# A hybrid attention / mLSTM / HGRN2 backbone in two layers: a 32-byte tile at the right-hand end of SBUF

## The chip, the core and the metric

The kernel runs on one core of one Trainium2 chip. The metric is the device time of one execution in microseconds (us). Three runs of the kernel before took 3481.38, 3482.13 and 3482.68 us; their median, 3482.13 us, is the time before.

## The reference

Two layers over 1024 latent tokens and 256 context tokens of width 1024, in fp32. Cut to what matters here:

```python
def reference(x, c, ctx, c_ctx, ...):
    for l in range(DEPTH):                      # DEPTH = 2
        need_ctx = l < DEPTH - 1
        shift, scale, gate = _ada(c, w_ada[l], b_ada[l])
        h_lat = _rms(x, norm_w[l]) * (1.0 + scale) + shift
        h_ctx = _rms(ctx, norm_w[l]) * (1.0 + scale_c) + shift_c
        if l % 2 == 0:      # neighbourhood attention || bidirectional mLSTM
            y_lat, y_ctx = _ab_mixer(h_lat, h_ctx, w_in_ab[j], ...)   # h @ w_in, heads, ... @ w_out
        else:               # bidirectional HGRN2, 16 heads
            y_lat, y_ctx = _c_mixer(h_lat, h_ctx, w_in_c[j], ...)
        x = x + gate * y_lat
        if need_ctx:
            ctx = ctx + gate_c * y_ctx
    return x
```

Each mixer projects the normed and modulated stream `h` (1280 x 1024) onto 9,232 or 10,240 columns, works on the heads, and projects the result back with `w_out`.

## The kernel before

**Split matmuls.** Each large product is made of three: a matrix is split into a high part rounded to the fp32r type and a low part that holds the rest (`split`, L70 to L73: ScalarE writes the high part, VectorE the low one). `dense` (L125 to L131) issues per 128 rows of the contraction high x high (L128), high x low (L129) and low x high (L130), or the like, into one PSUM bank; `out_sum` (L829 to L837) does the same for the output projections (L835 to L837). Each of these matmuls has a stationary operand of 128 x 128 (loaded by an LDWEIGHTS of its own) and a moving operand of 128 x 256 or 128 x 512. In the profile's rows the moving operand stands first behind the arrow: `mm<-hh,wh` streams `hh` past a stationary `wh`.

**Two ends of SBUF.** Tiles come from pools. [...] Right-hand are:

- `hh` and `hl` (`open_h`, L251 to L254), the two parts of `h`, 40,960 bytes each, in both layers;
- pool `oy` (L1289 in layer 0, L1375 in layer 1) for the output projections: weight slabs `wol`, `woh`, the parts of the activations `yl`, `yh`, staging tiles `woraw` and `wraw`, sums `oacc`;
- pool `w1` (L1332), the ring of weight slabs `wl`, `wh` of layer 1.

Left-hand are the ring of layer 0 (`wl`, `wh` in pool `w0`), `wxl`, `wxh` of the wide projections, `wgl`, `wgh` of the gates, `wzl`, `wzh` of layer 1 (pool `hg`), the slabs of pool `wo1` (`wol`, `woh` of the last stages and of the second half of layer 0's output projection), and all tiles of the heads.

As the program is built, every right-hand tile begins 32 bytes behind a multiple of 64 (`hh` of layer 0 at byte 147,424, `hl` at 188,384). The left-hand weight slabs begin at multiples of 64, and so do the slices of them that matmuls read. (Some left-hand tiles of the attention begin 32 bytes behind one; the change leaves them there.) So a matmul that streams a left-hand slab past a stationary slice of `hh`, or the other way round, has one operand at a multiple of 64 and one 32 bytes behind; in this text such a matmul is called **mixed**. One with both operands on one side is called **same**.

**Stages**, in us from the start of the profiled execution:

- 0 to 265: modulation, `hh` and `hl`, first projections, gates;
- 265 to 1105: neighbourhood attention, with the projections of the next heads (`na_qk`, `na_z`, `proj_out`, `proj_out_tr`) between its small matmuls. `proj_nat` (L134) holds a slice of `hh` and streams the weights, 256 wide; `proj_tr` (L143) holds the weights and streams `hh`, 512 wide for the latents, 256 for the context. All of them are mixed;
- 1105 to 1590: mLSTM, with wide projections (`proj_wide`, L275: weights streamed 512 wide, mixed) laid between;
- 1590 to 1865: output projection of layer 0. In its first part six of eight slabs are left-hand and the activations right-hand (mixed), two slabs right-hand (same); later all is same;
- 1865 to 3277: HGRN2 over 16 heads. `hg_proj` (L882) streams `hh` past slabs of pool `w1`, both right-hand (same); `hg_vz` (L912) streams `wzl`, `wzh` past `hh`, 256 wide (mixed); the rest is left-hand;
- 3277 to 3481: output projection of layer 1, at first same, then with slabs of `wo1` (mixed, L1400 to L1406).

**Order.** The order of the instructions on each engine is laid down when the program is built. In `build` (L1154) the constants are loaded first; L1219 opens the right-hand stack with `hh` and `hl`.

Of the kernel before, what the change touches and what calls it, by code (L numbers as in the profile page):

```python
# [9 lines left out]
F32 = mybir.dt.float32  # L10
# [8 lines left out]
P = 128  # L19
# [25 lines left out]
class Prog:  # L45
# [1108 lines left out]
    def build(self):  # L1154
        tc, nc, a = self.tc, self.nc, self.a
        dma = nc.sync.dma_start
        with ExitStack() as es:
# [58 lines left out]
            )  # L1216


            right = ExitStack()  # L1219
            es.enter_context(right)  # L1220
            self.open_h(right)
# [76 lines left out]
            with tc.tile_pool(name="op0", bufs=2) as op, ExitStack() as wl:  # L1298
# [32 lines left out]
                right = es.enter_context(ExitStack())  # L1331
# [292 lines left out]
```

## Time and profile before

| | |
|---|---|
| median of three runs | 3482.13 us |
| span of the profiled execution, first to last instruction | 3480.9 us |
| TensorE (PE) busy | 3431.2 us, 99% |
| VectorE (DVE) busy | 2307.4 us, 66% |
| ScalarE (ACT) busy | 1488.6 us, 43% |
| GpSimd (POOL) busy | 725.6 us, 21% |

The span is that of one execution; what lies around it (launch and end) is 1.2 us if that execution was like the median one. A matmul's time in the profile is modelled from its start to the end of its pipeline, so matmuls that follow each other overlap: what one costs in a stream is the time from its start to the start of the next, which the timeline gives. Rows of "one line's instructions" give minimum/median/maximum time of one in ns, then the first and the last start; rows of groups give the busy time, the mean of one, and the idle time before them.

### The profile page before, as it was taken

To read this page: it belongs to the slowest core of one execution; us is meant where nothing else is said; L and a number is where in the kernel's file an instruction comes from. 1 tells how busy PE (TensorE), PEld (TensorE's weight loads), DVE (VectorE), ACT (ScalarE), POOL (GpSimd) and SP (SyncE) were. 2 spreads that over 40 slices of the span, in tenths; PEclk is the share of its full clock that TensorE was granted. 3 is DMA by queue.
4 is the path that set the end of the run, shared out by engine and by line. 5 is a ranking of instruction groups with operands and counts; after the bars stand their busy time and mean duration, and the time that the engine had idled before them with its cause. 6 is when DMAs were issued, how large, how long until landed. Compare 5 with 4: busy or idle time off the path is not lost.

```text
span 3480.9 us, 60852 instructions
## 1 busy us (share of the span) xinstructions
PE 3431.2 (99%) x22668; PEld 3042.3 (87%) x22668; DVE 2307.4 (66%) x5447; ACT 1488.6 (43%) x3577; POOL 725.6 (21%) x1076
## 2 busy tenths in 40 slices
PE   8999999999999999999999999999999999999997
PEld 5779998889989888898888999999999999999876
DVE  4546665666655566787666676667677677666767
ACT  5445554554544444455354333333333333333442
POOL 2222222222111112221110122122223222111125
PEclk9999999999999999999999999999999999999999
DMA  5542222322233434444752111111112211111274
GB/s 205 173 132 59 81 76 74 91 79 75 79 87 99 147 117 127 133 128 148 223 158 68 49 58 55 56 58 58 58 55 64 64 59 57 41 34 34 83 233 154
DMA packets 331527, 333.34 MB, mean 96 GB/s; under 512 B 30984, under 2 KB 277960, under 8 KB 331232
## 3 DMA queue, kind: packets, MB, share of 16 engines
q1 hardware_dynamic: 291008, 222.76, 21.7%
q0 software_dynamic: 40224, 106.69, 9.0%
q8 instruction: 179, 2.93, 0.4%
q14 instruction: 116, 0.95, 0.1%
HBM read 259.40 MB, written 69.79 MB: 95 GB/s over the span
## 4 chain that ended last, share of the span: by engine, by line
PE 89%; DVE 3%; issue 3%; DMA 2%; ACT 1%; POOL 1%; SPq 0%; POOLq 0%; ACTq 0%; DVEq 0%
PE mm L128 18%; PE mm L129 18%; PE mm L130 18%; PE s L1028 5%; PE mm L835 3%; PE mm L836 3%; PE mm L837 3%; PE acc L775 2%; PE tr L755 2%; PE acc L547 2%; PE s L556 2%; PE acc L537 1%; PE acc L1090 1%; PE acc L1088 1%; PE acc L1089 1%
## 5 line engine op out<-in xcount | busy, mean ns | idle before, releaser
L129 PE MATMUL mm<-hl,wh 128*128 128x512 f32 (+1 forms) x1600 | 587.1, 367 | 0.0
L128 PE MATMUL mm<-hh,wh 128*128 128x512 f32 (+1 forms) x1600 | 584.3, 365 | 0.0
L130 PE MATMUL mm<-hh,wl 128*128 128x512 f32 (+1 forms) x1600 | 583.7, 365 | 0.0
L128 PE MATMUL mm<-wh,hh 128*128 128x256 f32 (+1 forms) x1520 | 471.2, 310 | 1.2 <-ACT ev L317 0.6
L129 PE MATMUL mm<-wl,hh 128*128 128x256 f32 (+1 forms) x1520 | 469.9, 309 | 0.0
L130 PE MATMUL mm<-wh,hl 128*128 128x256 f32 (+1 forms) x1520 | 469.0, 309 | 0.3 <-DVE hl L262 0.3
L130 PEld LDWEIGHTS mm<-hh,wl 128*128 128x128 f32 x1600 | 301.6, 189 | 45.0 <-issue 0.5
L128 PEld LDWEIGHTS mm<-hh,wh 128*128 128x128 f32 x1600 | 301.4, 188 | 44.6 <-issue 0.3
L129 PEld LDWEIGHTS mm<-hl,wh 128*128 128x128 f32 x1600 | 301.6, 189 | 43.7 <-issue 0.2
L128 PE MATMUL mm<-wzh,hh 128*128 128x256 f32 x1024 | 299.7, 293 | 2.3 <-DVE gq L909 1.4
L128 PEld LDWEIGHTS mm<-wh,hh 128*128 128x128 f32 x1520 | 286.5, 189 | 16.0 <-issue 1.1
L129 PEld LDWEIGHTS mm<-wl,hh 128*128 128x128 f32 x1520 | 286.5, 188 | 14.7 <-issue 3.0
L130 PEld LDWEIGHTS mm<-wh,hl 128*128 128x128 f32 x1520 | 286.4, 188 | 13.8 <-issue 1.5
L130 PE MATMUL mm<-wzh,hl 128*128 128x256 f32 x1024 | 292.3, 285 | 0.0
L129 PE MATMUL mm<-wzl,hh 128*128 128x256 f32 x1024 | 292.0, 285 | 0.0
L72 ACT CAST wh<-wraw 128x512 fp32r<-128x512 f32 x240 | 147.3, 619 | 233.0 <-PE mm L129 175.8
L73 DVE TENSOR_TENSOR wl<-wraw,wh 128x512 fp32r<-128x512 f32 x240 | 164.8, 691 | 89.6 <-ACT wh L72 80.4
L1023 ACT COPY gksel<-gK 128x512 f32<-128x512 f32 x192 | 120.0, 633 | 218.2 <-PE s L1028 127.3
L1028 PE MATMUL s<-gQ,gksel 128*128 128x128 f32 x1536 | 203.9, 276 | 0.4 <-ACT gksel L1023 0.4
L128 PEld LDWEIGHTS mm<-wzh,hh 128*128 128x128 f32 x1024 | 193.4, 189 | 3.8 <-DVE gq L909 2.4
L129 PEld LDWEIGHTS mm<-wzl,hh 128*128 128x128 f32 x1024 | 193.6, 189 | 0.0
L130 PEld LDWEIGHTS mm<-wzh,hl 128*128 128x128 f32 x1024 | 192.7, 188 | 0.0
(400 smaller groups left out, 8017.5 us busy)
## 6 DMA issues: line engine op xcount, KB each, us to landing
wraw<-in_wab_dram SPq DMA_DIRECT2D x112, 256.0 KB
wraw<-in_wc_dram SPq DMA_DIRECT2D x96, 256.0 KB
wraw<-yd SPq DMA_DIRECT2D x94, 256.0 KB
adar<-in_wada_dram POOLq DMA_DIRECT2D x32, 512.0 KB, 4.4
wraw<-in_wc_dram SPq DMA_DIRECT2D x128, 128.0 KB
md<-ev POOLq DMA_DIRECT2D x60, 256.0 KB, 2.8
mloz<-md SPq DMA_DIRECT2D x40, 256.0 KB
adar<-in_wada_dram SPq DMA_DIRECT2D x16, 512.0 KB
```

The costliest lines, as they stand in the source:

```text
L72: nc.scalar.copy(hi, x)
L73: nc.vector.tensor_tensor(out=lo, in0=x, in1=hi.bitcast(F32), op=ALU.subtract)
L128: mm(ps, lhsT=lh(k), rhs=rh(k), start=(start and k == 0), stop=False)
L129: mm(ps, lhsT=lh(k), rhs=rl(k), start=False, stop=False)
L130: m = mm(ps, lhsT=ll(k), rhs=rh(k), start=False, stop=(stop and k == nk - 1))
L547: nc.tensor.matmul(num, lhsT=qc[:, j, :], rhs=C[d][:, j, :], start=False, stop=(j == 1))
L556: nc.tensor.matmul(u, lhsT=st["k"][c][:, j * P : (j + 1) * P], rhs=vw, start=True, stop=True)
L835: mm(ps, lhsT=yh[k], rhs=w.h(kk), start=(kk == 0), stop=False)
L836: mm(ps, lhsT=yh[k], rhs=w.l(kk), start=False, stop=False)
L837: mm(ps, lhsT=yl[k], rhs=w.h(kk), start=False, stop=(kk == 8 * len(qs) - 1))
L1023: nc.scalar.copy(ksel.rearrange("p (b s i) -> p b s i", s=2, i=h), pick(K))
L1028: nc.tensor.matmul(pa[:, c, :].rearrange("p (b s i) -> p b s i", s=2, i=h), lhsT=ksel[:, c * P : (c + 1) * P], rhs=qp[:, c * nbc : (c + 1) ...
```

## The change

Before `hh` and `hl` are opened, a pool `edge` on the right-hand side takes one tile of 8 fp32 (32 bytes) in each partition, for the whole program, and VectorE sets it to zero. Nothing reads it.

```diff
@@ -1216,6 +1216,8 @@
             )
 
 
+            edge = es.enter_context(tc.tile_pool(name="edge", bufs=1, side="right"))
+            nc.vector.memset(self.t(edge, [P, 8], F32, "edge"), 0.0)
             right = ExitStack()
             es.enter_context(right)
             self.open_h(right)
```

In the built program every other right-hand tile begins 32 bytes lower (`hh` of layer 0 at 147,392, `hl` at 188,352), at a multiple of 64; no left-hand tile moves. On each engine the same instructions stand in the same order, but for the one MEMSET more, the second instruction of work on VectorE. The waits are the same, with VectorE's count one higher.

## The prediction

> **What bounds the kernel now.** First the page: span, TensorE's busy time, and the chain of waits that ended last.
>
> ```profile
> span 3480.9 us, 60852 instructions
> PE 3431.2 (99%) x22668; PEld 3042.3 (87%) x22668; DVE 2307.4 (66%) x5447; ACT 1488.6 (43%) x3577; POOL 725.6 (21%) x1076
> PE 89%; DVE 3%; issue 3%; DMA 2%; ACT 1%; POOL 1%; SPq 0%; POOLq 0%; ACTq 0%; DVEq 0%
> PE mm L128 18%; PE mm L129 18%; PE mm L130 18%; PE s L1028 5%; PE mm L835 3%; PE mm L836 3%; PE mm L837 3%; PE acc L775 2%; PE tr L755 2%; PE acc L547 2%; PE s L556 2%; PE acc L537 1%; PE acc L1090 1%; PE acc L1088 1%; PE acc L1089 1%
> ```
>
> TensorE has 89% of the chain, 54% on the three lines of `dense` and 9% on those of `out_sum`. Next the busy times by stage (from:to, length, then PE, PEld, DVE, ACT, POOL busy, granted clock, DMA share, GB/s).
>
> ```profile
> 0.00:1590.00 1590.00, 1571.81 (x10814) 1368.47 (x10814) 979.47 (x2929) 769.31 (x1938) 346.79 (x586) 1.00 0.36 109
> 1590.00:1700.00 110.00, 107.51 (x482) 88.86 (x483) 79.74 (x200) 54.73 (x122) 14.98 (x26) 1.00 0.59 182
> 1700.00:1865.00 165.00, 164.01 (x783) 136.64 (x782) 100.93 (x229) 82.33 (x201) 16.85 (x36) 1.00 0.51 158
> 1865.00:3277.00 1412.00, 1409.31 (x9785) 1306.47 (x9784) 997.87 (x1877) 500.59 (x1162) 279.44 (x377) 1.00 0.17 52
> 3277.00:3481.00 204.00, 178.54 (x810) 141.82 (x807) 149.41 (x212) 81.63 (x156) 67.54 (x51) 0.96 0.63 197
> ```
>
> In every stage but the last TensorE is busy all but 1 to 2% of the time, at the full clock. So what matters of a change of addresses is whether matmuls that read right-hand tiles stream faster or slower.
>
> **The change part by part.** *The MEMSET* is the one new instruction. It comes between these two on VectorE:
>
> ```profile
> 0.80 0.07 DVE L1177 MEMSET mhalf<- 128x8 f32 x1 [0.80 <-PEq L1612]
> 2.75 0.18 DVE L1199 TENSOR_SCALAR sct<-sct 128x16 f32<-128x16 f32 x1 [1.88 <-ACT sct L1198]
> ```
>
> The same shape took 0.07 us, and VectorE then waits 1.88 us for ScalarE, which waits for a load. That hides it: 0. Without that cover, 0.07 us.
>
> *Who reads and writes right-hand tiles besides TensorE.* Splits into them are ScalarE casts; here one kind with all tiles left (`wzh`) and one with all right (`wh<-woraw`):
>
> ```profile
> L72 ACT CAST wzh<-wraw x64: 618/621/645, 1868.4 to 3200.1; 128x512 fp32r<-128x512 f32 x64
> L72 ACT CAST wh<-woraw x8: 616/622/627, 3283.1 to 3337.5; 128x512 fp32r<-128x512 f32 x8
> ```
>
> 621 and 622 ns: no difference of sides, so 0. DMAs into right-hand tiles (`woraw`, part of `wraw`) belong to the 2% that DMA has of the chain; no row tells their rate from that of others, and I take 0. PSUM isn't touched.
>
> *512-wide mixed matmuls.* Here the rows do differ. L836 by tile in three stretches (1590 to 1700, 1700 to 1865, 3360 to 3470), minimum/median/maximum in ns:
>
> ```profile
> L836 PE MATMUL mm<-wol,yh x57: 387/389/580, 1601.5 to 1700.0; 128*128 128x512 f32 x57
> L836 PE MATMUL mm<-wl,yh x54: 392/396/587, 1593.3 to 1672.1; 128*128 128x512 f32 x54
> ```
>
> ```profile
> L836 PE MATMUL mm<-wol,yh x182: 389/389/398, 1700.0 to 1844.5; 128*128 128x512 f32 x182
> L836 PE MATMUL mm<-wl,yh x20: 392/396/480, 1738.1 to 1846.8; 128*128 128x512 f32 x20
> ```
>
> ```profile
> L836 PE MATMUL mm<-wol,yh x129: 389/397/628, 3359.7 to 3469.5; 128*128 128x512 f32 x129
> L836 PE MATMUL mm<-wl,yh x4: 389/389/389, 3360.4 to 3362.4; 128*128 128x512 f32 x4
> ```
>
> Six groups of one line and one shape. In the first stretch `wl` is a left-hand slab under right-hand `yh` (mixed, 396) and `wol` right-hand (same, 389), and both take turns inside one accumulation. In the last the names change places: `wol` is left-hand (mixed, 397), `wl` right-hand (same, 389). So it is neither the tile nor the stage. Same on the left (most of the x182) and same on the right (x4) are both 389, so it isn't that a start 32 bytes off is slow in itself: the two operands' places within 64 bytes agree or they don't. After the change all of them agree.
>
> The price comes from the starts in unbroken streams; the first and last row of each: 40 matmuls with both sides left, then 32 mixed ones with `hh`:
>
> ```profile
> 1728.54 0.40 PE L836 MATMUL mm<-wol,yh 128*128 128x512 f32 x1
> ...
> 1737.42 0.39 PE L836 MATMUL mm<-wol,yh 128*128 128x512 f32 x1
> ```
>
> ```profile
> 258.68 0.39 PE L128 MATMUL mm<-hh,wh 128*128 128x512 f32 x1
> ...
> 265.90 0.39 PE L129 MATMUL mm<-hl,wh 128*128 128x512 f32 x1
> ```
>
> 8.88 us over 39 steps is 227.7 ns, 7.22 over 31 is 232.9: 5.2 ns less for each mixed one. How many there are (each row stands for three lines):
>
> ```profile
> L128 PE MATMUL mm<-wh,hh 128*128 128x256 f32 x1280 | 371.8, 291 | 1.2 <-ACT ev L317 0.6 <-ACT ev L634 0.3 <-ACT hh L261 0.2
> L128 PE MATMUL mm<-hh,wh 128*128 128x512 f32 x384 | 152.5, 397 | 0.0
> L128 PE MATMUL mm<-wh,hh 128*128 128x512 f32 x240 | 99.4, 415 | 0.0
> L128 PE MATMUL mm<-hh,wh 128*128 128x256 f32 x192 | 54.0, 281 | 0.0
> L128 PE MATMUL mm<-wxh,hh 128*128 128x512 f32 x80 | 32.5, 408 | 0.0
> ```
>
> ```profile
> L128 PE MATMUL mm<-wzh,hh 128*128 128x256 f32 x1024 | 299.7, 293 | 2.3 <-DVE gq L909 1.4 <-ACT gEc L921 0.5 <-ACT gz L934 0.4
> L128 PE MATMUL mm<-hh,wh 128*128 128x512 f32 x752 | 298.1, 396 | 0.0
> L128 PE MATMUL mm<-hh,wzh 128*128 128x256 f32 x128 | 35.9, 281 | 0.0
> ```
>
> The first fence is 0 to 1590 us, the second 1865 to 3277. Mixed and 512 wide: (384 + 240 + 80) x 3 = 2112 in layer 0, (54 + 20) x 3 = 222 in its output projection, 129 x 3 = 387 in the last stage: 2721, x 5.2 ns = **14.1 us less**. The ends: the x752 of HGRN2 are same already and yet have a mean of 396 like the mixed x384 (397), since other matmuls break their streams; if the attention's matmuls do that to layer 0 as well, nothing is gained. If each gains the whole 397 to 389, it is 21.8 us. I take 5.2: the unbroken stream of layer 0 is the row nearest to what changes.
>
> *256-wide mixed matmuls* are 7872: (1280 + 192 + 1024 + 128) x 3. Streams, first and last row: 75 rows of weights past `hh` (mixed), 23 of `hh` past weights (mixed), 19 in HGRN2 with both right (same), 63 of `wz` past `hh` (mixed):
>
> ```profile
> 276.98 0.28 PE L130 MATMUL mm<-wh,hl 128*128 128x256 f32 x1
> ...
> 285.74 0.28 PE L129 MATMUL mm<-wl,hh 128*128 128x256 f32 x1
> ...
> 270.43 0.28 PE L129 MATMUL mm<-hl,wh 128*128 128x256 f32 x1
> ...
> 272.99 0.28 PE L130 MATMUL mm<-hh,wl 128*128 128x256 f32 x1
> ...
> 2032.74 0.28 PE L129 MATMUL mm<-hl,wh 128*128 128x256 f32 x1
> ...
> 2034.89 0.28 PE L129 MATMUL mm<-hl,wh 128*128 128x256 f32 x1
> ...
> 1893.22 0.28 PE L130 MATMUL mm<-wzh,hl 128*128 128x256 f32 x1
> ...
> 1900.66 0.28 PE L129 MATMUL mm<-wzl,hh 128*128 128x256 f32 x1
> ```
>
> Per step: 8.76/74 = 118.4, 2.56/22 = 116.4, 2.15/18 = 119.4, 7.44/62 = 120.0 ns. Here agreement is no gain: if all come to 119.4, the 3840 of weights past `hh` lose 1.0 each (3.8 us), the 576 the other way round 3.0 (1.7 us), the 3072 with `wz` gain 0.6 (1.8 us), and the 384 `hh,wz`, for which I take 3.0 too, lose 1.2 us: **4.9 us more**. The ends: 0.6 gained by all (4.7 us less) and 3.0 lost by all (23.6 us more).
>
> *Sum.* 14.1 - 4.9 = 9.2 us less for TensorE. TensorE has 89% of the chain and what it saves elsewhere is met by other waits, so 8.2 us less of the span: 3480.9 to 3472.7. The median of the runs shown lies 1.2 us above this execution's span; with that, 3474 us. Between the ends of the two terms lie 26.5 us less and 23.6 us more.
>
> [...]
>
> **The rivals.**
>
> *Both at a multiple of 64 is better still than both behind it.* Then HGRN2's 752 x 3 matmuls, same before, would gain too: from a mean of 396 to the 389 of the x182, 7 ns, 15.8 us more. For it: the purest row is left-hand. Against: `wl,yh` x4, right-hand, has 389 as well, and broken streams explain the 396. With the sum: 0.89 x (9.2 + 15.8) = 22.3 us less, 3460 us; if half of it is so, 3467.
>
> *Nothing changes.* The 7 ns come from something that goes with the sides but isn't the place within 64 bytes, say the distance between the two operands; then the change doesn't do what it says: 3482 us. For it: no row has a right-hand tile at a multiple of 64. Against: the exchange of names above.
>
> *Slower: the 256-wide streams pay.* Operands that agree hold the 256-wide matmul at a longer period, and it is the more frequent form. If each of the 7872 loses the 3.0 ns that lie between 116.4 and 119.4, 23.6 us come in, mostly in the attention and in `hg_vz`, against 14.1 gained: 0.89 x 9.5 = 8.5 us more, 3491 us. It decides from 14.1 / 7872 = 1.8 ns each. For it: the 19 same ones have 119.4. Against: the `wz` streams (3072) are at 120.0 already.
>
> **How the numbers follow.** A difference under about 0.2% (7 us) is what a measurement of this kernel can't tell from no change. The forecast, 3474 us, has 0.62, with a range of its own of 3467 to 3480; its middle lies just beyond 7 us, but a share of the first rival's gain would add to it, so 0.45 of that is faster and 0.17 within. The first rival has 0.15 (faster), no change 0.09, slower 0.14. Faster 0.60, within 0.26, slower 0.14. The range of 3460 to 3486 takes in the first rival, no change and the near part of the third; it leaves out the third's own time and the outermost ends.
>
> **What would show it.** Right: L836's medians at 389 in all stretches, the stream near 258 us at about 228 ns a step, `mm<-hh,wh` x384 well under a mean of 397. The 256-wide streams near 277 us at 119 to 120 shows the toll; at 118.4 or less there is none. `wz` at 120.0 as before. Wrong: medians of 396 that stay; the x752 falling too (first rival); 256-wide steps over 120.2, 1.8 above 118.4 (third); or TensorE's busy time falling while the chain's share of DMA or VectorE grows by as much.

## The result, and the profile after

| | before | after |
|---|---|---|
| median of 19 runs each (us) | 3482.68 | 3476.21 |
| lowest to highest | 3479.62 to 3486.51 | 3471.94 to 3480.69 |
| span of the profiled execution | 3480.9 | 3472.7 |

The ratio of the times is 0.998, with a 95% interval of 0.9974 to 0.9986: 6.5 us less, a gain of 0.2% whose interval lies clear of no change. One execution among the experiments, the first profiled one of `minus64`, ran at a granted clock of 0.65 and took 4837 us; it is left out of the times below. From the page of the changed kernel, the span and the busy times:

```profile
span 3472.7 us, 60853 instructions
...
PE 3425.1 (99%) x22668; PEld 3046.3 (88%) x22668; DVE 2308.0 (66%) x5448; ACT 1486.9 (43%) x3577; POOL 727.0 (21%) x1076
```

TensorE is busy 6.1 us less than before and the span is 8.2 us shorter; VectorE, ScalarE and GpSimd each changed by less than 2 us. So the time went where it was looked for, in TensorE's matmuls. Next, where along the execution. The rows of two lines, first before, then after; "from to" are the first and the last start (L708: last small matmuls of the attention; L1028: HGRN2):

```profile
L708 PE MATMUL s<-akl,aqs x160: 278/282/386, 301.9 to 1141.2; 128*128 128x256 f32 x160
L1028 PE MATMUL s<-gQ,gksel x1536: 270/275/388, 1889.9 to 3279.6; 128*128 128x128 f32 x192
```

```profile
L708 PE MATMUL s<-akl,aqs x160: 274/283/385, 302.2 to 1140.7; 128*128 128x256 f32 x160
L1028 PE MATMUL s<-gQ,gksel x1536: 270/275/387, 1887.0 to 3272.1; 128*128 128x128 f32 x192
```

And L836 of the changed kernel in the first of the three stretches that the prediction shows (1590 to 1700 us), and in the last, here from 3340 to 3470 us, where the kernel before has a median of 397 as well:

```profile
L836 PE MATMUL mm<-wol,yh x60: 389/389/589, 1599.3 to 1699.5; 128*128 128x512 f32 x60
L836 PE MATMUL mm<-wl,yh x54: 389/394/587, 1591.2 to 1669.5; 128*128 128x512 f32 x54
```

```profile
L836 PE MATMUL mm<-wol,yh x136: 389/394/628, 3344.9 to 3461.2; 128*128 128x512 f32 x136
L836 PE MATMUL mm<-wl,yh x8: 389/389/389, 3347.6 to 3355.1; 128*128 128x512 f32 x8
```

The starts give the gain by stage, each beside the forecast for TensorE that the prediction's terms add up to:

| | how far earlier at its end | gained in it | forecast |
|---|---|---|---|
| to the end of the attention (last L708) | 0.5 us | 0.5 | |
| mLSTM, to the first L836 with `wl,yh` (1593.3, then 1591.2) | 2.1 | 1.6 | 5.5 for both |
| output projection of layer 0 (first L1028) | 2.9 | 0.8 | 1.2 |
| HGRN2 (last L1028) | 7.5 | 4.6 | 0.6 |
| last stage (last L836: 3469.5, then 3461.2) | 8.3 | 0.8 | 2.0 |

So the total was about right, but its place was not: more than half came in HGRN2, where almost nothing was forecast. L836 shows why the last stage gained less than forecast: the median of the slabs of `wo1` went from 397 to 394 ns, not to 389.

Groups of one shape of the changed kernel (busy us, mean ns), of 0 to 1590 us and of HGRN2:

```profile
L128 PE MATMUL mm<-wh,hh 128*128 128x256 f32 x1280 | 373.9, 292 | 1.0 <-ACT ev L317 0.6 <-ACT ev L634 0.3
L128 PE MATMUL mm<-hh,wh 128*128 128x512 f32 x384 | 151.0, 393 | 0.0
L128 PE MATMUL mm<-wh,hh 128*128 128x512 f32 x240 | 98.7, 413 | 0.2 <-ACT wh L72 0.2
```

```profile
L128 PE MATMUL mm<-wzh,hh 128*128 128x256 f32 x1024 | 299.5, 292 | 2.1 <-DVE gq L909 1.2 <-ACT gEc L921 0.5 <-ACT gz L934 0.4
L128 PE MATMUL mm<-hh,wh 128*128 128x512 f32 x748 | 296.1, 396 | 0.0
```

The mean of the x384 fell from 397 to 393 and that of the x240 only from 415 to 413. The 752 of HGRN2 (748 of them start in this window) stay at 396: the first rival did not happen. The streams of the prediction, again by the first and the last start (`hh` past `w`, `w` past `hh`, `wz` past `hh`):

```profile
258.80 0.40 PE L128 MATMUL mm<-hh,wh 128*128 128x512 f32 x1
...
265.85 0.39 PE L129 MATMUL mm<-hl,wh 128*128 128x512 f32 x1
...
276.87 0.28 PE L129 MATMUL mm<-wl,hh 128*128 128x256 f32 x1
...
285.98 0.28 PE L130 MATMUL mm<-wh,hl 128*128 128x256 f32 x1
...
1890.28 0.28 PE L130 MATMUL mm<-wzh,hl 128*128 128x256 f32 x1
...
1897.76 0.28 PE L130 MATMUL mm<-wzh,hl 128*128 128x256 f32 x1
```

7.05 us over 31 steps is 227.4 ns (232.9 before), 9.11 over 76 is 119.9 (118.4 before), 7.48 over 63 is 118.7 (120.0 before). These are single clean streams. For whole stages the following table has the mean time from a matmul's start to the next start, over all of that form that are followed within 260 ns (512 wide) or 150 ns (256 wide), worked out from the starts in both traces; below it is called the step.

| form, stage | steps | before | after |
|---|---|---|---|
| 512 wide, `h` past `w`, attention | 975 | 233.3 | 228.9 |
| 512 wide, `w` past `h`, mLSTM | 450 | 232.9 | 229.9 |
| 512 wide, `wo1` past `y`, last stage | 349 and 341 | 234.2 | 233.4 |
| 512 wide, `h` past `w`, HGRN2 | 2112 and 2099 | 229.5 | 228.9 |
| 256 wide, `w` past `h`, attention | 2143 and 2146 | 118.4 | 119.7 |
| 256 wide, `h` past `w`, attention | 504 | 117.3 | 119.5 |
| 256 wide, `wz` past `h`, HGRN2 | 2854 | 119.8 | 118.7 |

### The profile page after: what moved, and what is told of

Same layout as the page of the kernel before. It is cut to its first block, busy times and chain, and to the rows that moved or that the text cites. A ratio compares the mean times of both kernels' runs of the same rounds, so it can differ in the third digit from the quotient of the medians.

```text
span 3472.7 us, 60853 instructions
## 1 busy us (share of the span) xinstructions
PE 3425.1 (99%) x22668; PEld 3046.3 (88%) x22668; DVE 2308.0 (66%) x5448; ACT 1486.9 (43%) x3577; POOL 727.0 (21%) x1076
## 4 chain that ended last, share of the span: by engine, by line
PE 88%; issue 3%; DVE 3%; DMA 2%; ACT 1%; POOL 1%; SPq 0%; POOLq 0%; ACTq 0%; DVEq 0%
PE mm L128 18%; PE mm L129 18%; PE mm L130 18%; PE s L1028 5%; PE mm L835 3%; PE mm L836 3%; PE mm L837 3%; PE acc L775 2%; PE tr L755 2%; PE acc L547 2%; PE s L556 2%; PE acc L537 1%; PE acc L1089 1%; PE acc L1088 1%; PE acc L1090 1%
## 5 line engine op out<-in xcount | busy, mean ns | idle before, releaser
L129 PE MATMUL mm<-hl,wh 128*128 128x512 f32 (+1 forms) x1600 | 586.2, 366 | 0.0
L128 PE MATMUL mm<-hh,wh 128*128 128x512 f32 (+1 forms) x1600 | 582.8, 364 | 0.0
L130 PE MATMUL mm<-hh,wl 128*128 128x512 f32 (+1 forms) x1600 | 582.0, 364 | 0.0
L128 PE MATMUL mm<-wh,hh 128*128 128x256 f32 (+1 forms) x1520 | 472.6, 311 | 1.2 <-ACT ev L317 0.6
L129 PE MATMUL mm<-wl,hh 128*128 128x256 f32 (+1 forms) x1520 | 471.6, 310 | 0.0
L130 PE MATMUL mm<-wh,hl 128*128 128x256 f32 (+1 forms) x1520 | 471.0, 310 | 0.0
L130 PEld LDWEIGHTS mm<-hh,wl 128*128 128x128 f32 x1600 | 301.9, 189 | 43.3 <-issue 0.2
L128 PEld LDWEIGHTS mm<-hh,wh 128*128 128x128 f32 x1600 | 301.9, 189 | 43.1 <-issue 0.5
L129 PEld LDWEIGHTS mm<-hl,wh 128*128 128x128 f32 x1600 | 302.0, 189 | 41.6 <-issue 0.2
L128 PEld LDWEIGHTS mm<-wh,hh 128*128 128x128 f32 x1520 | 290.0, 191 | 15.3 <-issue 1.1
L129 PEld LDWEIGHTS mm<-wl,hh 128*128 128x128 f32 x1520 | 289.9, 191 | 14.3 <-issue 2.6
L128 PE MATMUL mm<-wzh,hh 128*128 128x256 f32 x1024 | 299.5, 292 | 2.1 <-DVE gq L909 1.2
L130 PEld LDWEIGHTS mm<-wh,hl 128*128 128x128 f32 x1520 | 290.0, 191 | 12.9 <-issue 1.5
L130 PE MATMUL mm<-wzh,hl 128*128 128x256 f32 x1024 | 292.2, 285 | 0.0
L129 PE MATMUL mm<-wzl,hh 128*128 128x256 f32 x1024 | 291.8, 285 | 0.0
L1023 ACT COPY gksel<-gK 128x512 f32<-128x512 f32 x192 | 119.9, 633 | 215.4 <-PE s L1028 118.8
L1028 PE MATMUL s<-gQ,gksel 128*128 128x128 f32 x1536 | 204.1, 276 | 0.2 <-ACT gksel L1023 0.2
L128 PEld LDWEIGHTS mm<-wzh,hh 128*128 128x128 f32 x1024 | 193.5, 189 | 3.5 <-DVE gq L909 2.2
L129 PEld LDWEIGHTS mm<-wzl,hh 128*128 128x128 f32 x1024 | 193.5, 189 | 0.0
L130 PEld LDWEIGHTS mm<-wzh,hl 128*128 128x128 f32 x1024 | 193.1, 189 | 0.0
```

Source lines behind the costliest of these rows:

```text
L128: mm(ps, lhsT=lh(k), rhs=rh(k), start=(start and k == 0), stop=False)
L129: mm(ps, lhsT=lh(k), rhs=rl(k), start=False, stop=False)
L130: m = mm(ps, lhsT=ll(k), rhs=rh(k), start=False, stop=(stop and k == nk - 1))
L1023: nc.scalar.copy(ksel.rearrange("p (b s i) -> p b s i", s=2, i=h), pick(K))
L1028: nc.tensor.matmul(pa[:, c, :].rearrange("p (b s i) -> p b s i", s=2, i=h), lhsT=ksel[:, c * P : (c + 1) * P], rhs=qp[:, c * nbc : (c + 1) ...
```

## The experiments

The starts within 128 bytes may explain what the table leaves odd, the `wo1` slabs' small gain (234.2 to 233.4 ns): after the change the layer-0 slabs and `hh` both begin 64 bytes behind a multiple of 128, but the slabs of `wo1` begin at a multiple of 128 and the activations 64 behind one. The start addresses here and below are those in the built programs. In all of them the uppermost right-hand tile ends at byte 229,344 (`hl` of the kernel before: 188,384 + 40,960), and each pool with `side="right"` lies below those that are open when it is opened, so a tile opened first moves all that come after it. There were four theories to begin with. A: the operands' places within 64 bytes must agree (the prediction's). B: within 128 bytes. C: right-hand tiles must begin at multiples of 64. D: any shift, or the MEMSET, does it. Each ratio below is against runs of the kernel before on the same chip.

**64 bytes in place of 32 (edge64).**

```diff
-            nc.vector.memset(self.t(edge, [P, 8], F32, "edge"), 0.0)
+            nc.vector.memset(self.t(edge, [P, 16], F32, "edge"), 0.0)
```

> The tile at the right-hand end has 64 bytes in place of 32: right-hand tiles begin 32 bytes behind a multiple of 64 as before, only 64 bytes lower than before; left-hand slabs are unmoved, so the mixed matmuls are mixed again. Theory A (the two operands' places within 64 bytes must agree) and theory B (their places within 128 bytes must agree): the 512-wide streams of layer 0 are back at 233 ns a step, L128 mm<-hh,wh of 265 to 1590 us back from a median of 389 to 393 or more, L836 mm<-wol,yh of the last stage at 396 or 397, and the time within 2 us of before, 3482.7. Theory C (what counts is that each right-hand tile begins at a multiple of 64): the same. Theory D (any shift, or the MEMSET itself, brings the gain): 3476 as in the changed kernel, medians of 389. One thing is open in A and B: the weights that stream past hh 256 wide now stand 32 bytes ahead of hh within 128, where before they stood 32 bytes short of it (before: 118.4 ns a step); the few that already had the operand that streams 32 ahead (hh past weights) took 116.4 to 117.4. If the sign matters to the 6912 matmuls of that form, 1 ns each is 7 us less, and the streams show it.

Measured: 3469.89 us, ratio 0.9963 (0.9951 to 0.9976). The 512-wide streams went back to 233 as A, B and C have it (`h` past `w` in the attention 232.9), so D falls. But the time is lower than that of the changed kernel, by the 256-wide streams. That of `w` past `hh`:

```profile
275.00 0.28 PE L129 MATMUL mm<-wl,hh 128*128 128x256 f32 x1
...
283.87 0.28 PE L130 MATMUL mm<-wh,hl 128*128 128x256 f32 x1
```

8.87 us over 76 steps is 116.7 ns, against 118.4 before and 119.9 after. The mean steps are 117.1 for `w` past `h` and 117.6 for `wz` past `h` (119.8 before): 3840 x 1.3 and 3072 x 2.2 ns are 11.8 us. The open point in the expectation was the larger effect: it matters whether the streamed operand lies 32 bytes ahead of the other or 32 short of it (the sign, below; for `w` past `h` 117.1 against 118.4 ns), which neither A nor B has.

**96 bytes (edge96).** The same line with [P, 24].

> The tile at the right-hand end has 96 bytes: right-hand tiles begin at multiples of 128, so at multiples of 64 as in the changed kernel, but the slabs of layer 0 and wz begin 64 bytes behind a multiple of 128, and the slabs of the last stage at a multiple of 128. Theory A (agreement within 64) and theory C (right-hand tiles at multiples of 64): as the changed kernel everywhere, 3476 us, L128 mm<-hh,wh of 265 to 1590 us at a median of 389, L836 mm<-wol,yh of the last stage at 394. Theory B (agreement within 128): the two trade places. Layer 0 is back at about 233 ns a step and a median of 393 or more, and the last stage falls from 394 to 389; 2100 matmuls lose what the change gave them and 400 gain, so the time lies at 3480 to 3484, unless the 256-wide streams take a step of their own at this distance. Theory D (any shift): 3476.

Measured: 3460.53 us, ratio 0.9934 (0.9920 to 0.9947), 22 us less than before. Streams, and L836 in the last stage:

```profile
257.38 0.39 PE L128 MATMUL mm<-hh,wh 128*128 128x512 f32 x1
...
264.61 0.39 PE L129 MATMUL mm<-hl,wh 128*128 128x512 f32 x1
...
275.37 0.28 PE L129 MATMUL mm<-wl,hh 128*128 128x256 f32 x1
...
283.98 0.28 PE L130 MATMUL mm<-wh,hl 128*128 128x256 f32 x1
```

```profile
L836 PE MATMUL mm<-wol,yh x136: 389/389/632, 3331.4 to 3445.4; 128*128 128x512 f32 x136
```

7.23 us over 31 steps is 233.2 ns: layer 0 lost its gain although every right-hand tile begins at a multiple of 64, and the last stage has 389 at last. For these two B is right and A and C are wrong. The time that B gave is wrong, by the reservation that stood with it: 8.61 over 76 is 113.3 ns for the 256-wide stream. Over whole stages `wz` past `h` fell to 115.3 and `w` past `h` to 117.2: 3072 x 4.5 and 3840 x 1.2 ns are 18.4 of the 22 us. For `w` past `h` a distance of 64 bytes is better than 0 (117.2 against 119.6 ns over all stages of the changed kernel).

**32 bytes on the left instead (left32).**

```diff
+            nc.vector.memset(self.t(cp, [P, 8], F32, "edge"), 0.0)
             right = ExitStack()
```

> No tile at the right-hand end; instead a 32-byte tile among the constants, so that every left-hand tile behind it moves up by 32 bytes and the right-hand ones stay where they were before. All operands of the mixed matmuls now begin 32 bytes behind a multiple of 64. Theories A and B (only agreement counts): as the changed kernel, 3476 us, L128 mm<-hh,wh of 265 to 1590 us at 389, and the last stage still at 394 since its slabs stand 64 bytes apart from the activations within 128. Theory C (a multiple of 64 is needed): no gain, 3482.7 or slower, medians of 393 or more. Theory D: 3476, with no pattern by stage.

Measured: 3476.27 us, ratio 0.9983 (0.9974 to 0.9991), as the changed kernel. The group of `h` past `w`, 512 wide, of 0 to 1590 us:

```profile
L128 PE MATMUL mm<-hh,wh 128*128 128x512 f32 x384 | 151.0, 393 | 0.0
```

The same 393 as after, with both operands 32 bytes behind a multiple of 64, and the last stage at 394 too. C falls: the gain came with the difference of the two places, not with either place.

**All dense matmuls at distance 0 within 128 bytes (all0).**

```diff
+                nc.vector.memset(self.t(pool, [P, 16], F32, "pad", 1), 0.0)
                 self.na_values(1, pool)
...
             with tc.tile_pool(name="op0", bufs=2) as op, ExitStack() as wl:
+                nc.vector.memset(self.t(op, [P, 16], F32, "pad", 1), 0.0)
...
                 wl1 = wl.enter_context(tc.tile_pool(name="wo1", bufs=1))
+                nc.vector.memset(self.t(wl1, [P, 16], F32, "pad", 1), 0.0)
```

> The changed kernel with three more tiles of 64 bytes in the left-hand pools (before the wide projection of the gates stage, in front of the second output projection of layer 0, in front of the slabs of the last stage), so that all dense matmuls have both operands at the same place within 128 bytes. Theory A (64 is enough): as the changed kernel, 3476 us, L836 mm<-wol,yh of the last stage stays at a median of 394. Theory B (128): this median falls to 389, the 504 matmuls concerned (384 of them in the last stage) lose about 5 ns each, 2 to 3 us in all: 3473 to 3475. A tile that moves by 64 bytes has no other price that the trace shows.

Measured: 3475.20 us, ratio 0.9976 (0.9967 to 0.9985). L836 in the last stage:

```profile
L836 PE MATMUL mm<-wol,yh x144: 387/389/632, 3328.7 to 3465.3; 128*128 128x512 f32 x144
```

394 became 389, as B has it. In the time, 1 us less than after is inside the intervals; the row shows the effect, the time doesn't settle it.

**wz alone (wz64).** The question was now whether 64 bytes between the operands make the 256-wide form fast (E), or the place of the right-hand tiles (F).

```diff
-            whole = [self.t(pool, [P, ns, 512], F32R, tag + c, 1) for c in "lh"]
+            x = 128 if tag == "wz" else 0
+            whole = [
+                self.t(pool, [P, ns * 512 + x], F32R, tag + c, 1)[:, x // 8 : x // 8 + ns * 512].rearrange(
+                    "p (s f) -> p s f", f=512
+                )
+                for c in "lh"
+            ]
```

> The changed kernel in which only wzl and wzh are moved, by 64 bytes (a view that begins 64 bytes into a slab that is 512 bytes longer); hh and hl stay. Theory E (256-wide matmuls run fastest when the streamed operand and the weights lie 64 bytes apart, slowest when they agree): HGRN2's streams of wz past hh fall from 118.8 ns a step to the 115.3 of the kernel with 96 bytes, all else stays; 3072 x 3.5 ns x 0.89 is 9.6 us, so 3467 us. Theory F (the gain of the 96 bytes came from right-hand tiles at multiples of 128, not from a distance): wz stays at 118.8 and the time at 3476.

Measured: 3465.46 us, ratio 0.995 (0.9938 to 0.9963), 11 us less than the changed kernel's median. The stream (six lines lower in the file, so L136 is L130):

```profile
1891.26 0.28 PE L136 MATMUL mm<-wzh,hl 128*128 128x256 f32 x1
...
1898.41 0.28 PE L136 MATMUL mm<-wzh,hl 128*128 128x256 f32 x1
```

7.15 us over 63 steps is 113.5 ns (118.7 after); the mean step is 115.1, and the forms without `wz` are as after. F falls, and E's forecast holds: 115.3 was expected.

**128 bytes (edge128).** The line of the first two experiments with [P, 32].

> The tile at the right-hand end has 128 bytes: every right-hand tile 128 bytes lower than before. Theory B (places within 128 bytes decide): no difference from before, 3482.7 us, 512-wide streams of layer 0 at 233 ns a step, w past hh at 118.4, wz past hh at 120.0. If the pattern is longer than 128 bytes, the 256-wide streams show other values (w stands 96 bytes ahead of hh now, before it stood 32 behind it).

Measured: 3482.34 us, ratio 0.9996 (0.9987 to 1.0005): the time of before, as B says. The streams say otherwise:

```profile
279.02 0.28 PE L129 MATMUL mm<-wl,hh 128*128 128x256 f32 x1
...
288.12 0.28 PE L130 MATMUL mm<-wh,hl 128*128 128x256 f32 x1
...
1901.63 0.28 PE L130 MATMUL mm<-wzh,hl 128*128 128x256 f32 x1
...
1909.08 0.28 PE L130 MATMUL mm<-wzh,hl 128*128 128x256 f32 x1
```

9.10 over 76 is 119.7 ns for `w` (118.4 before), 7.45 over 63 is 118.3 for `wz` (120.0 before). The two forms have exchanged their values, and 3840 x 1.2 ns more (4.7 us) hides 3072 x 1.6 ns less (4.9 us). In layer 0 the distance of `w` from `hh` went from 224 to 96 bytes within 256, and that of `wz` from 96 to 224. So the pattern is longer than 128 bytes, and B falls for this form; the exchange fits a length of 256, as do distances that differ by 256: `w` here, 96 bytes ahead of `hh`, has 119.6 over all stages, and `wz` before, 352 ahead within 512, had 119.8. The 512-wide streams, at 233 to 234, can't tell. An unchanged total was two changes that cancel.

**hh and hl 64 bytes apart (hsplit).** Does a step go with the matmul's own weights or with those that are loaded meanwhile? The next weights are loaded while a stream runs: in the kernel before, the LDWEIGHTS of L129 begins at 258.68 us as L128's matmul does, and that of L130 at 258.91 us as L129's does.

```diff
+        self.nc.vector.memset(self.t(self.hpool, [P, 16], F32, "pad", 1), 0.0)
         self.hl = self.t(self.hpool, [P, KD, T], F32R, "hl", 1)
```

> The changed kernel with a 64-byte tile between hh and hl, so that hh begins 64 bytes lower than in the changed kernel and hl stays. In the streams of wz (and of w, 256 wide) past h, three lines take turns: L128 streams past hh while hh is loaded for L129, L129 streams past hh while hl is loaded for L130, L130 streams past hl while the next hh is loaded. Theory G (the stream collides with the weights that are being loaded meanwhile): steps begun by L129 are slow (118.8 for wz, 119.6 for w), those begun by L128 and L130 fast (115.3 and 117). Theory H (a matmul's own two operands matter): those begun by L130 are slow, those of L128 and L129 fast. By both the 512-wide matmuls that stream hh past slabs at the old place go to 233 ns and those that stream hl stay at 227 to 229. Time by the sum of these, 9.9 us more for the 512-wide and 17 less for the 256-wide: about 3470; it doesn't tell G from H.

Measured: 3481.74 us, ratio 0.9996 (0.9987 to 1.0005), not 3470. Mean steps in ns by the line that begins them:

| form, stage | L128 | L129 | L130 |
|---|---|---|---|
| 256 wide, `w` past `h`, attention | 116.5 | 117.4 | 119.8 |
| 256 wide, `wz` past `h`, HGRN2 | 118.9 | 119.5 | 116.5 |
| 512 wide, `h` past `w`, attention | 234.4 | 234.9 | 229.9 |

H fits the first row, and neither fits the other two. In the second, the steps of L128 and L129, at distance 192, are slow, and that of L130, at 128, is not. In the third, streams of `hl` (L129), at distance 0, are slow and those of `hh` in L130, at 192, are not; the sum of the three is as if all stood at 192, so HGRN2's 2304 `h` past `w` gave back 4.4 ns each (10 us), where 7 us had been counted. The larger part of the miss is `wz`: the mean of its three steps is 118.3, 0.4 ns under the changed kernel, 1.3 us over 3072, where two thirds of them at 115.3 would have been 7 us. Two operand places in one accumulation are not the sum of the two cases. What collides, and whether anything does, stays open.

**The other sign, everywhere (minus64).** `lbm` goes, and `wz` moves by 128 bytes in its slabs (x // 4 in place of x // 8 in the edit of wz).

```diff
-            mx = self.t(cp, [P, 16], F32, "lbm")
+            mx = self.lb[:, 0, :]
```

> The changed kernel, in which the 64-byte tile lbm among the constants is gone (its place is taken by a half of lb that isn't in use yet) and wzl, wzh lie 128 bytes further into their slabs: the layer-0 slabs and wz begin 64 bytes below hh within 512, where in the kernel with 96 bytes the layer-0 slabs began 64 above it. Theory I (the sign counts: below is better for 256-wide weights that stream past h, above better for 512-wide): w past hh falls from 117 to about 115.3 (3840 matmuls), h past w 512 wide from 233 to 230 (1152), against 3 ns more for the 720 of w past hh 512 wide and 2 for the 576 of h past w 256 wide; 7 us less than with 96 bytes, x 0.89: 3454. Rival: the 115.3 belongs to wz and its stage, not to the sign; then w stays at 117 and the time at 3460 or a few us above.

Measured: ratio 0.9933 (0.9919 to 0.9946), 3458.5 to 3461.8 us in four executions. The steps come from a second profile of the same kernel.

> The same kernel as minus64, whose profile fell into an execution at a granted clock of 0.65 and tells nothing of the streams. Theory I: w past hh 256 wide at 115.3 ns a step (117 with 96 bytes), h past w 512 wide at 230 (233 with 96 bytes). Since the time, 3461 us, is that of the kernel with 96 bytes and not the 3454 forecast, at least one of the two must fail, or a stage lose by as much: the rival has w at 117 and h past w at 233.

Measured: 3460.02 us, ratio 0.9932 (0.9914 to 0.9950). Both halves of I hold: `w` past `h` in the attention has 115.7 and `h` past `w` 230.1. The loss is elsewhere: `wz` past `h` at 116.5, where wz64 had 115.1 with `wz` and `h` at the very same addresses. Here are two streams of one place in HGRN2, first of this kernel and then of the last experiment below:

```profile
1890.65 0.28 PE L135 MATMUL mm<-wzl,hh 128*128 128x256 f32 x1
...
1893.24 0.28 PE L136 MATMUL mm<-wzh,hl 128*128 128x256 f32 x1
```

```profile
1893.70 0.28 PE L135 MATMUL mm<-wzl,hh 128*128 128x256 f32 x1
...
1896.20 0.28 PE L136 MATMUL mm<-wzh,hl 128*128 128x256 f32 x1
```

Each has 22 steps: 117.7 and 113.6 ns. At this distance a stream takes one of two values, and the mean of a stage says how many took which. Counted over the 63 accumulations of `wz` past `h` of 24 matmuls each that run nearly unbroken, 38 have 113.3 to 114.2 and 25 have 117.6 to 117.9 in wz64, against 21 and 42 in minus64_again; none lies between. Is that chance? Two kernels were profiled once more for it.

> The kernel of wz64 once more. wz and hh stood at the same addresses there and in minus64_again, yet wz past hh took 115.1 ns a step in the one and 116.4 in the other. If the step varies from execution to execution, it may be anything between these here; if what else moved by 64 bytes in the left-hand pools makes the difference, it is 115.1 again (within 0.2).

> The changed kernel once more, for the same question: its streams repeat within 0.2 ns (w past hh 256 wide in the attention 119.7, wz past hh 118.7, hh past w 512 wide in the attention 228.9), or they vary by a nanosecond between executions and single steps can't be read so finely.

Measured: 3466.11 and 3474.59 us. Every mean step named repeats within 0.1 ns (`wz` 115.1 and 118.7, `w` 119.7, `h` past `w` 228.9). So it is not chance from execution to execution; the program decides.

**Layer 1 as in wz64 (minus64_l1).** What had moved with `minus64` besides was every other left-hand tile of layer 1.

```diff
             lk = self.fp = l1.enter_context(tc.tile_pool(name="hgk", bufs=1))
+            nc.vector.memset(self.t(lk, [P, 16], F32, "pad", 1), 0.0)
```

> minus64 with a 64-byte tile at the start of layer 1's left-hand pools and wz only 64 bytes into its slabs: layer 0 is as in minus64, and every tile of layer 1 stands where it stands in wz64. If the place of the other tiles made wz past hh slow in minus64 (116.4 against 115.1 ns a step), it is 115.1 to 115.2 again, w past hh of the attention stays at 115.5 to 115.7 and h past w 512 wide at 230; 3072 x 1.3 ns and 2304 x 0.6 ns, x 0.89, is 4.8 us less than 3460: 3455 to 3457. If the layer-0 edit does it in another way, wz stays at 116.4 and the time at 3460.

Measured: 3455.51 us, ratio 0.9922 (0.9909 to 0.9936), the fastest of all, 27 us less than before, and some 20 under the changed kernel's median. `wz` is back at 115.2, `h` past `w` of HGRN2 at 228.8 (229.6 in minus64_again). The split of `wz` is 37 and 26 again. So the streams also depend on the place of tiles that TensorE doesn't read in these matmuls; which of them, and by what way, wasn't tried.

## Why the prediction was right in the total, and where it was wrong

Put together by distance (start of the streamed operand less that of the weights, within 256 bytes), the mean steps of the matmuls of `dense` and `out_sum` in nine kernels (before, after, edge64, edge96, left32, all0, wz64, edge128, minus64_l1), all stages of a kernel pooled; lowest and highest kernel, where it has over 100 steps at that distance:

| distance | 512 wide, ns | 256 wide, ns |
|---|---|---|
| 0 | 228.3 to 229.0 | 119.0 to 119.5 |
| 32 | 233.0 to 233.2 | 117.1 to 117.3 |
| 64 | 230.1 | 117.2 to 117.8 |
| 96 | 233.3 | 119.6 to 119.8 |
| 128 | 232.8 (one kernel) | 118.7 |
| 160 | 233.9 to 234.1 | 117.6 to 118.1 |
| 192 | 233.0 to 233.2 | 115.1 to 115.5 |
| 224 | 232.8 to 233.0 | 118.3 to 118.4 |

Pooled, a distance has nearly one value in all nine. Two things limit the table. Within a distance single stages differ, most at 0 for 512 columns (227.0 to 230.3), and the means of 256 columns at 64 and 192 mix the two values of a stream: in edge96, 17 of 76 accumulations of `w` past `h` have 113.5 and the others 117.5 to 118. And two kernels that are left out don't fit: minus64_again has 116.1 at 192, and hsplit, the one kernel with `hh` and `hl` at different places, has 118.9 at 192, 116.4 at 128 and, 512 wide, 231.2 at 0. So the distance gives the step where both parts of a split lie at the same one; it is not shown to be the mechanism. With the table, the steps of the prediction:

*MEMSET, VectorE, ScalarE, DMA at 0:* right. Neither edge64 (`h` past `w` in the attention at 232.9 ns) nor edge128 (512-wide streams at 233 to 234), which have the MEMSET too, brings the gain in the 512-wide streams.

*"The two operands' places within 64 bytes agree or they don't":* right that it is relative (left32), too coarse in its length. The change put most matmuls to distance 0, but `wo1` and two smaller groups to 64 or 192, and `wz` to 128.

*512 wide, 14.1 us:* mis-sized. The clean stream gave what was forecast (5.5 ns less, forecast 5.2). Over whole stages it was 4.3 for `h` past `w` (1152), 2.9 for `w` past `h` (720), 2.3 for the wide slabs (240), and 0.8 in the last stage (387), where the distance went from 160 to 192: 5.0 + 2.1 + 0.6 + 0.3, with 0.5 from the output projection of layer 0 (162 x 3.2), is 8.5 us. So the term was mis-sized by taking one of the cleanest streams for all, and the last stage by the 64 bytes.

*256 wide, 4.9 us more:* 3840 lost 1.2 and 576 lost 2.2 (forecast 1.0 and 3.0), 4.6 + 1.3 us. But "all come to 119.4" failed for `wz`: its distance went from 96 to 128, not to 0, and it gained 1.1 each, 3.4 us, where 0.6 was forecast; `h` past `wz` lost 0.8, not 3.0. Together 2.8 us more.

*HGRN2's `h` past `w`, forecast unchanged:* 0.6 ns less each, 1.3 us. That isn't the first rival: left32 has the same 228.9 with both operands off the multiple of 64. An effect of other tiles like that in minus64_l1 would fit, but this case of it wasn't tried.

*Sum:* 8.5 - 2.8 + 1.3 = 7.0 us less for TensorE, against 9.2 forecast. By stage the steps agree with the starts: in HGRN2 they give 3.4 - 0.3 + 1.3 = 4.4 of the 4.6 us. The factor of 0.89 can't be judged: the medians differ by 6.5, the profiled spans by 8.2, since the execution profiled after the change, at 3474.44 us, was one of the shorter ones. A gain too large by 5.6 stood against a toll too large by 2.1 and a missing 1.3: that the total came out near is in part luck. The 1.2 us added at the end should have been 1.7 to 1.8, the time of an execution less its span (3474.44 less 3472.7, 3469.89 less 3468.1).

*The chances:* 0.60 stood on a gain of over 7 us and 0.26 on a smaller one or none; the measured 6.5 us lie just within the second, though their interval is clear of no change.

*The rivals:* both at a multiple of 64, no (x748 at 396, left32). Nothing changes, no; but its example, the distance between the operands, is what the step goes with in nine of the eleven kernels. Slower by the 256-wide streams: the toll existed, but at 1.2 ns for the 3840 instead of the 3.0 for all, below the 1.8 from which it decides, and the 3072 with `wz` gained.

*What would show it:* the stream near 258 us (227.4) and the x384 (393) came as said, and the chain's shares of DMA and VectorE stayed at 2% and 3%. Medians of 389 in all stretches did not (394), nor `wz` at 120.0 (118.7): the two signs that pointed past 64 bytes.

## What to carry to other kernels

Where TensorE sets the time with split matmuls of a load each, look at the start addresses of the streamed operand and the weights within 256 bytes, and measure the step (start to start) by form; here 512-wide streams were fastest at distance 0 or 64 (228.3 to 230.1 ns a step, 232.8 to 234.1 at the others), 256-wide ones at 192 (115.1 to 115.5, 117.1 to 119.8 at the others), with both parts of a split at the same place, and a few shifts of 32 to 128 bytes were worth 27 us, four times what the first guess brought. Take the price of a form from all its steps in the stage that changes, not from the cleanest stream of one. And read the steps of every form even where the total doesn't move: in edge128 a gain and a loss of 5 us hid each other.

## What was unexpected of the hardware

In the nine kernels of the table, all with both parts of a split at the same place, the step went with the distance of the two operands within 256 bytes and with its sign, by up to 3% for 512 columns (228.3 ns at 0, 234.1 at 160) and 4% for 256 (115.1 to 115.5 at 192, 117.2 to 117.8 at 64, 119.8 at 96). At a distance of 192 a single stream of `wz` past `h` had about 113.6 or 117.7 ns. The mean over the stage repeats from execution to execution (115.1 in wz64 and in wz64_again), and the place of tiles that TensorE doesn't read there, moved by 64 bytes, changes it (116.5 in minus64_again, 115.2 in minus64_l1).
